# A two-layer retention and attention backbone: its first stage taken feature block by feature block

## The chip, the cores and the metric

The kernel runs on one core of one Trainium2 chip. The metric is the device time of one execution in microseconds (us). Three executions of the kernel before took 2027.63, 2028.96 and 2029.16 us; their median, 2028.96 us, is what the changed kernel is compared with.

Five engines work side by side, each on its own queue of instructions in order: TensorE (PE in the profile, with its weight loads shown apart as PEld), VectorE (DVE), ScalarE (ACT), GpSimd (POOL) and SyncE (SP), which here issues nearly all the transfers (DMAs). [...]

## The reference, cut to what matters

The program is two layers of a diffusion backbone over 256 latent tokens and 256 context tokens, 2048 features each. Layer 0 is a retention with 8 heads, layer 1 a windowed attention. Each layer first normalises its input and modulates it with a shift and a scale that come from a product of SiLU(c) with a large matrix `ada_w`:

```python
c_act = jax.nn.silu(c)
cc_act = jax.nn.silu(c_ctx)
for i in range(DEPTH):
    mod_l = c_act @ ada_w[i] + ada_b[i]
    mod_c = cc_act @ ada_w[i] + ada_b[i]
    sh_l, sc_l, gt_l = jnp.split(mod_l, 3, axis=-1)
    sh_c, sc_c, gt_c = jnp.split(mod_c, 3, axis=-1)
    h_l = _rms_norm(x, norm_gain[i]) * (1 + sc_l[:, None]) + sh_l[:, None]
    h_c = _rms_norm(ctx, norm_gain[i]) * (1 + sc_c) + sh_c
    ...
```

The change lies in the first stage of layer 0. There `h` (512 tokens by 2048 features) is made, and the queries and keys of heads 0 and 1 are projected from it. Retention also needs powers of each head's decay, which come from two vectors of 8 logits.

## The kernel before

**Tiling.** Features lie on partitions: 16 feature blocks (`kb`) of 128 features, 512 tokens in the free dimension (0 to 255 latent, 256 to 511 context). `xT` is the input in this form, `hT_h` and `hT_l` are the modulated input split into a high part and a rest. Every large product is three products (`mm3`, lines 124 to 128): high by high, high by rest, rest by high. Weights arrive by `load_w` (lines 117 to 122): a DMA of 512 KB into one of three buffers `wraw`, a cast on ACT that gives `wh` (line 107) and a subtraction on DVE that gives `wl` (line 104).

**Order.** The kernel is written in a framework that keeps the data dependencies and puts each engine's instructions in an order of its own: what was written earlier goes first among what its planner takes to be ready. So the order in the source is a priority, not a sequence, and each engine's queue may mix work from several places. `tc.issue_after(ins)` adds an edge: whatever the block puts on the engine of `ins` is queued behind `ins`.

**The first stage (lines 243 to 359).** SP issues the eight loads of `xT` (512 KB each, line 247) and the packed constants `cst` (line 248). DVE and POOL work out the decays (lines 256 to 287): some thirty small DVE instructions and three powers on POOL. ACT squares the 16 blocks of `xT`, DVE adds the squares up (lines 290 to 297, two buffers `sq`), and `token_rstd` (lines 192 to 204) turns the sum into one factor per token: PE sums over partitions (line 198), DVE and POOL take the power (lines 183 and 189), PE spreads it (line 203), ACT copies it to `rB` (line 299).

Shift and scale come in "strips". A unit is two feature blocks; its matrix columns arrive in four quarters of 1 MB, `araw` (four buffers, line 314). A quarter is four products with only 32 columns of weights each, in full fp32, side by side in the four column groups of PE (line 316). After the fourth quarter ACT copies the sums out (line 321), PE turns them (line 325), DVE adds up the column groups and adds bias and gain (lines 328, 221 and 224), and `modulate` (lines 206 to 215) makes `hT_h` and `hT_l` of both blocks.

The loop of lines 340 to 356 takes eight groups of products per unit: four output blocks `j` of head 0 (c = 0, accumulated over all units in four PSUM tiles `qk0`) and four of head 1 (c = 1, summed in SBUF in `qk1` through ACT or DVE, lines 354 and 356). PSUM has five `acc` tiles, four of which `qk0` holds, and three `pm` tiles; c = 1 uses the one left for `j` = 0 to 2 and a `pm` for `j` = 3. `DUE` puts the four quarters of the next unit ahead of groups 0, 2, 4 and 5 of the unit at hand.

**Behind it.** The eight heads follow (from line 386), each with projections and tasks put between their pieces. The decays are first read in `decays(h)` (lines 460 to 473), by PE on line 463 and by POOL on line 472, a power over 128 by 128 elements.

## Time and profile before

| | us |
|---|---|
| median of three executions | 2028.96 |
| span of the profiled execution | 2027.2 |
| PE busy in it | 1992.9 |
| DVE, ACT, POOL busy | 1151.6, 694.5, 227.5 |
| first instruction of PE | 20.3 |
| first product of the projections | 34.45 |
| last sum into `qk1` (line 356) starts | 161.9 |

The profile shows one execution. A row of a timeline or chain gives the start and the length of a piece of work in us, the engine, the line of the source and the tile written; what stands in brackets is idle time before it and what ended that. `x8` after a row means eight instructions merged. For line 316 one product is two instructions, so a quarter is `x8`.

### The profile page before, as it was taken

How to read it: one execution, taken by the hardware profiler on the slowest of the kernel's cores; microseconds unless marked ns; L12 is line 12 of the kernel's file. 1: busy time of each engine (PE TensorE's matmuls, PEld its weight loads, DVE VectorE, ACT ScalarE, POOL GpSimd, SP SyncE). 2: the span in 40 equal slices, each digit the busy share in tenths (PEclk: the TensorE clock that was granted, in tenths of full speed). 3: DMA queues.
4: the chain of work that ended last, by engine and by line, in shares of the span. 5: the costliest groups of instructions: out<-in, count | busy, mean ns of one | idle time of the engine just before them, and what ended most of it. 6: DMA issues, size and time to landing. Idle time of an engine off the chain costs nothing.

```text
span 2027.2 us, 25622 instructions
## 1 busy us (share of the span) xinstructions
PE 1992.9 (98%) x9776; PEld 1649.8 (81%) x9776; DVE 1151.6 (57%) x2299; ACT 694.5 (34%) x1043; POOL 227.5 (11%) x76
## 2 busy tenths in 40 slices
PE   5999999999999999999999999999999999999999
PEld 2558888888888888888888888888888788889999
DVE  4556323778678688686464254333232665777754
ACT  3224223232232232232232234322221434656643
POOL 6500402203104004004000000000000010000000
PEclk9999999999999999999999999999999899999999
DMA  9873224555556556655654325533333234444446
GB/s 362 332 266 109 93 89 146 183 191 177 182 177 192 172 180 182 186 180 166 203 173 164 114 94 166 186 126 123 105 125 103 95 109 148 143 135 133 145 161 198
DMA packets 113290, 330.15 MB, mean 163 GB/s; under 512 B 12176, under 2 KB 18448, under 8 KB 108944
## 3 DMA queue, kind: packets, MB, share of 16 engines
q1 hardware_dynamic: 103952, 315.94, 48.0%
q10 hardware_dynamic: 9216, 12.59, 1.7%
q8 instruction: 76, 1.25, 0.2%
q14 instruction: 46, 0.38, 0.1%
HBM read 315.90 MB, written 12.58 MB: 162 GB/s over the span
## 4 chain that ended last, share of the span: by engine, by line
PE 94%; DMA 2%; DVE 2%; ACT 1%; issue 1%; POOL 0%; SPq 0%; ACTq 0%; DVEq 0%; POOLq 0%
PE acc L126 28%; PE acc L127 27%; PE acc L128 27%; PE pm L126 2%; PE pm L127 2%; PE pm L128 2%; PE pm L316 2%; DMA wraw<-in_wo 1%; DMA wraw<-uT_d 1%; DVE wl L104 1%; PE pm L756 1%; PE pm L530 1%; ACT wh L107 1%; DVE ssq L297 0%; DMA xT<-in_xT 0%
## 5 line engine op out<-in xcount | busy, mean ns | idle before, releaser
L104 DVE TENSOR_TENSOR wl<-wraw,wh 128x1024 fp32r<-128x1024 f32 x368 | 449.6, 1223 | 649.6 <-ACT wh L107 649.4
L107 ACT CAST wh<-wraw 128x1024 fp32r<-128x1024 f32 x368 | 386.7, 1051 | 980.6 <-PE acc L128 489.5
L126 PE MATMUL acc<-wh,hT_h 128*128 128x512 f32 x1280 | 502.5, 393 | 1.1 <-ACT hT_h L212 1.1
L127 PE MATMUL acc<-wl,hT_h 128*128 128x512 f32 x1280 | 499.4, 390 | 0.0
L128 PE MATMUL acc<-wh,hT_l 128*128 128x512 f32 x1280 | 499.0, 390 | 0.0
L126 PE MATMUL acc<-hT_h,wh 128*128 128x512 f32 (+1 forms) x1264 | 443.5, 351 | 2.6 <-ACT wh L107 1.9
L127 PE MATMUL acc<-hT_l,wh 128*128 128x512 f32 (+1 forms) x1264 | 440.0, 348 | 0.0
L128 PE MATMUL acc<-hT_h,wl 128*128 128x512 f32 (+1 forms) x1264 | 435.5, 347 | 0.0
L409 DVE SCALAR_TENSOR_TENSOR ajunk<-abraw,crow 128x512 bf16<-128x512 f32 x448 | 308.3, 688 | 11.9 <-ACT crow L398 3.5
L126 PEld LDWEIGHTS acc<-hT_h,wh 128*128 128x128 f32 x1264 | 239.6, 190 | 54.7 <-DVE qk L356 7.2
L126 PEld LDWEIGHTS acc<-wh,hT_h 128*128 128x128 f32 x1280 | 241.2, 188 | 50.2 <-ACT hT_h L212 1.5
L128 PEld LDWEIGHTS acc<-wh,hT_l 128*128 128x128 f32 x1280 | 240.6, 188 | 50.3
L127 PEld LDWEIGHTS acc<-wl,hT_h 128*128 128x128 f32 x1280 | 241.1, 188 | 48.4 <-DVE wl L104 0.2
L127 PEld LDWEIGHTS acc<-hT_l,wh 128*128 128x128 f32 x1264 | 239.8, 190 | 32.2 <-issue 4.2
L128 PEld LDWEIGHTS acc<-hT_h,wl 128*128 128x128 f32 x1264 | 239.3, 189 | 31.0 <-issue 0.8
L472 POOL TENSOR_TENSOR dd<-two,dd 128x128 f32<-128x128 f32 x8 | 167.5, 20943 | 601.6 <-DVE dd L470 601.6
L189 POOL TENSOR_TENSOR rs<-ms,mhalf 128x1 f32<-128x1 f32 (+1 forms) x46 | 40.2, 874 | 1024.5 <-DVE ms L183 673.1
L126 PE MATMUL acc<-r_h,wh 128*128 128x512 f32 x176 | 68.5, 389 | 0.0
L127 PE MATMUL acc<-r_l,wh 128*128 128x512 f32 x176 | 68.5, 389 | 0.0
L128 PE MATMUL acc<-r_h,wl 128*128 128x512 f32 x176 | 68.5, 389 | 0.0
L127 PE MATMUL pm<-r_l,r_h 128*128 128x512 f32 (+1 forms) x176 | 65.7, 373 | 0.5 <-DVE r_l L104 0.5
L126 PE MATMUL pm<-r_h 128*128 128x512 f32 (+1 forms) x176 | 66.1, 375 | 0.0
(199 smaller groups left out, 1514.7 us busy)
## 6 DMA issues: line engine op xcount, KB each, us to landing
wraw<-in_w SPq DMA_DIRECT2D x272, 512.0 KB, 3.5
abraw<-in_adaB SPq DMA_DIRECT2D x256, 256.0 KB, 3.3
wraw<-in_wo SPq DMA_DIRECT2D x96, 512.0 KB, 3.5
araw<-in_adaS SPq DMA_DIRECT2D x32, 1024.0 KB, 7.3
uT_d<-ue ACTq DMA_DIRECT2D x32, 256.0 KB, 2.1
wraw<-uT_d SPq DMA_DIRECT2D x16, 512.0 KB, 3.8
xT<-in_xT SPq DMA_DIRECT2D x8, 512.0 KB, 8.5
wraw<-in_xT SPq DMA_DIRECT2D x8, 512.0 KB, 3.7
```

The source lines that it names most:

```text
L104: return nc.vector.tensor_tensor(out=out, in0=a, in1=hi.bitcast(F32), op=ALU.subtract)
L107: nc.scalar.copy(hi, src)
L126: nc.tensor.matmul(ps, lhsT=ah, rhs=bh, start=start, stop=False)
L127: nc.tensor.matmul(ps, lhsT=ah, rhs=bl, start=False, stop=False)
L128: nc.tensor.matmul(ps, lhsT=al, rhs=bh, start=False, stop=stop)
L189: nc.gpsimd.tensor_tensor(out=rs, in0=ms, in1=mhalf.to_broadcast([P, n]), op=ALU.pow)
L316: nc.tensor.matmul(ap_[32 * j:32 * j + 32, :n], lhsT=cpad[:, 4 * g + j, :], rhs=raw[:, j, :n], start=(g == 0), stop=(g == 3))
L409: nc.vector.scalar_tensor_tensor(out=junk, in0=raw, scalar=1.0, in1=crow[:, t, q * 512:(q + 1) * 512], op0=ALU.mult, op1=ALU.mult, accum_o ...
L472: nc.gpsimd.tensor_tensor(out=dd, in0=two.to_broadcast([P, P]), in1=dd, op=ALU.pow)
L530: nc.tensor.transpose(tp[:, q * P:(q + 1) * P], sg[:, q, f * P:(f + 1) * P], ident)
L756: nc.tensor.transpose(tp[:, j * P:(j + 1) * P], st["prob"][:, j, kb * P:(kb + 1) * P], ident)
```

## The change

It rewrites the first stage and the layout of one input; everything from line 361 on is untouched.

- The matrix for shift and scale is laid out by single feature block: `adaS_d[kb]` is 2 MB, in two halves of 1 MB. `ada_products(kb)` loads both halves and issues all 16 products of the block in a row, each over 256 columns instead of 512. `ada_finish(kb)` does the rest in the same PSUM tile.
- The products of block 0, with their two loads, stand ahead of the loads of `xT`, whose last pair is split into two single blocks. The finish of block 0 stands ahead of the squares.
- Block 0 is modulated straight from the PSUM tile of `token_rstd`; the copy to `rB` comes after. The first weights are loaded before that.
- The loop over 64 groups is written out: parts of head 0 (one block each, which is 12 products) and of head 1 (one block at first, then two) alternate with `ada(kb, after)`, whose products are queued on PE behind the last product of the part named.
- `cst` is loaded after the shift and scale weights of block 5 are asked for, and the decays are computed behind the modulation of block 5.

```diff
+        def ada_products(kb):
+            st = strips[kb] = m_tile()
+            for hf in range(2):
+                raw = pa.tile([P, 8, 256], F32, name="araw", tag="araw", bufs=4)
+                nc.sync.dma_start(out=raw, in_=adaS_d[kb, :, 8 * hf:8 * hf + 8, :])
+                for i in range(8):
+                    j = i % 4
+                    nc.tensor.matmul(st[32 * j:32 * j + 32, 0:L], lhsT=cpad[:, 8 * hf + i, :], rhs=raw[:, i, :],
+                                     start=(hf == 0 and i < 4), stop=(hf == 1 and i >= 4))
+
+        def ada_finish(kb):
+            st = strips.pop(kb)
+            ev = wide("ue", "ev", 2)
+            nc.scalar.copy(ev[:, :L], st[:, :L])
+            for b in range(2):
+                nc.tensor.transpose(st[:, L + b * P:L + (b + 1) * P], ev[:, b * P:(b + 1) * P], ident)
+            tv = pb.tile([P, 2, 2], F32, name="tv", tag="tv", bufs=2)
+            nc.vector.reduce_sum(tv, st[:, L:].rearrange("p (b g r) -> p b r g", b=2, g=4)[:, :, 0:2, :], axis=AX.X)
+            for kind in range(2):
+                ada_mod(kind, 0, kb, 1, tv[:, kind:kind + 1, :], sh0, gs0, gt0)
+
+        ada_products(0)
+        xT = pa.tile([P, KB, T], F32, name="xT")
+        for k0, nk in [(2 * i, 2) for i in range(7)] + [(14, 1), (15, 1)]:
+            nc.sync.dma_start(out=xT[:, k0:k0 + nk, :], in_=xT_d[:, k0:k0 + nk, :])
+        ada_finish(0)
...
+        w = {0: load_w(w0_d[0, 0])}
+        bp = token_rstd(pb, [ssq])
+        first_mod = modulate(wide("pt", "ht", 2), xT[:, 0, :], 0, gs0, sh0, bp)
         rB = wide("aacc0", "rB")
-        nc.scalar.copy(rB, token_rstd(pb, [ssq]))
+        nc.scalar.copy(rB, bp)
+
+        def ada(kb, after):
+            with tc.issue_after(after):
+                ada_products(kb)
+            ada_finish(kb)
+            last_mod[0] = modulate(wide("pt", "ht", 2), xT[:, kb, :], kb, gs0, sh0, rB)
...
+        ada(1, part(0, [0]))
+        with tc.issue_after(first_mod):
+            w[1] = load_w(w0_d[3, 0])
+        ada(2, part(1, [0]))
+        part(0, [1])
+        part(1, [1])
+        w[0] = load_w(w0_d[0, 1])
+        ada(3, part(0, [2]))
+        ada(4, part(0, [3]))
+        w[1] = load_w(w0_d[3, 1])
+        ada(5, part(1, [2, 3]))
+        nc.sync.dma_start(out=cst, in_=cst_d)
+        with tc.issue_after(last_mod[0]):
+            decay_powers()
+        for i in range(2, 8):
+            w[0] = load_w(w0_d[0, i])
+            part(0, [2 * i])
+            end = part(0, [2 * i + 1])
+            if i < 7:
+                ada(2 * i + 2, end)
+            w[1] = load_w(w0_d[3, i])
+            end = part(1, [2 * i, 2 * i + 1])
+            if i < 7:
+                ada(2 * i + 3, end)
```

`part(c, kbs)` issues, for the four output blocks `j`, the `mm3` of the blocks `kbs` and, for head 1, the sum into `qk1`, as the loop did; it returns the last product. `decay_powers()` holds lines 256 to 287 unchanged.

More of the change, by code (lines that the diff above doesn't have):

```diff
@@ L26 @@
 LOG2E = 1.4426950408889634
-DUE = (0, 2, 4, 5)
-DUE0 = (0, 2, 4, 5)
 GAP1, GAP2 = 4, 2
@@ L127, in mm3 @@
         nc.tensor.matmul(ps, lhsT=ah, rhs=bl, start=False, stop=False)
-        nc.tensor.matmul(ps, lhsT=al, rhs=bh, start=False, stop=stop)
+        return nc.tensor.matmul(ps, lhsT=al, rhs=bh, start=False, stop=stop).ins
     def gemm_ws(w_d, chunk, nkp, moving, n, hook=None, pre=None, tail=1):
@@ L212, in modulate @@
             nc.scalar.activation(hT_h[:, kb, c], t[:, c], AF.Identity, bias=sh[:, kb, s:s + 1])
-            nc.vector.scalar_tensor_tensor(out=hT_l[:, kb, c], in0=t[:, c], scalar=sh[:, kb, s:s + 1],
-                                           in1=hT_h[:, kb, c].bitcast(F32), op0=ALU.add,
-                                           op1=ALU.subtract)
+            last = nc.vector.scalar_tensor_tensor(out=hT_l[:, kb, c], in0=t[:, c], scalar=sh[:, kb, s:s + 1],
+                                                  in1=hT_h[:, kb, c].bitcast(F32), op0=ALU.add,
+                                                  op1=ALU.subtract)
+        return last.ins
     def ada_mod(kind, layer, k0, nk, src, sh, gs, gt, ntk=2):
@@ L241, in wide, with decay_powers @@
         return pb.tile([P, 512], F32, name=name, tag=tag, bufs=bufs)
-    with tc.tile_pool(name="pa", bufs=1) as pa:
-        xT = pa.tile([P, KB, T], F32, name="xT")
-        for i in range(8):
-            nc.sync.dma_start(out=xT[:, 2 * i:2 * i + 2, :], in_=xT_d[:, 2 * i:2 * i + 2, :])
-        nc.sync.dma_start(out=cst, in_=cst_d)
-        nc.scalar.activation(cact.rearrange("p k t -> p (k t)"), vec[:, V_C:V_C + 32], AF.Silu)
-        cpad = wide("aacc1", "cpad").rearrange("p (k t) -> p k t", t=32)
-        nc.gpsimd.memset(cpad, 0.0)
-        nc.vector.tensor_copy(cpad[:, :, 0:2], cact)
+    def decay_powers():
         xl = vec[:, V_LGT:V_LGT + 16]
@@ L287, in backbone @@
                                 in1=sixt.to_broadcast([P, 64]), op=ALU.mult)
+    with tc.tile_pool(name="pa", bufs=1) as pa:
+        cpad = wide("aacc1", "cpad").rearrange("p (k t) -> p k t", t=32)
+        nc.gpsimd.memset(cpad, 0.0)
+        nc.scalar.activation(cact.rearrange("p k t -> p (k t)"), vec[:, V_C:V_C + 32], AF.Silu)
+        nc.vector.tensor_copy(cpad[:, :, 0:2], cact)
+        strips, last_mod = {}, [None]
+        def ada_products(kb):
[22 more added lines that the diff above has]
+        ada_finish(0)
         ssq = wide("rows", "ssq")
@@ L297, in backbone @@
             nc.vector.tensor_tensor(out=ssq, in0=ssq, in1=sq, op=ALU.add)
+        w = {0: load_w(w0_d[0, 0])}
+        bp = token_rstd(pb, [ssq])
+        first_mod = modulate(wide("pt", "ht", 2), xT[:, 0, :], 0, gs0, sh0, bp)
         rB = wide("aacc0", "rB")
-        nc.scalar.copy(rB, token_rstd(pb, [ssq]))
-        units = [[2 * k, 2 * k + 1] for k in range(8)]
-        strips = {}
-        def strip_part(u, g):
-            kbs = units[u]
-            n, c0 = 256 * len(kbs), 256 * (kbs[0] % 2)
-            if g == 0:
-                strips[u] = m_tile()
-            ap_ = strips[u]
-            raw = pa.tile([P, 4, 512], F32, name="araw", tag="araw", bufs=4)
-            nc.sync.dma_start(out=raw[:, :, :n], in_=adaS_d[kbs[0] // 2, g][:, :, c0:c0 + n])
-            for j in range(4):
-                nc.tensor.matmul(ap_[32 * j:32 * j + 32, :n], lhsT=cpad[:, 4 * g + j, :],
-                                 rhs=raw[:, j, :n], start=(g == 0), stop=(g == 3))
-            if g < 3:
-                return
-            ev = wide("ue", "ev", 2)
-            nc.scalar.copy(ev[:, :n], ap_[:, :n])
-            tp = m_tile()
-            nb = n // P
-            for b in range(nb):
-                nc.tensor.transpose(tp[:, b * P:(b + 1) * P], ev[:, b * P:(b + 1) * P], ident)
-            tv = pb.tile([P, 2, 2, 2], F32, name="tv", tag="tv", bufs=2)
-            nc.vector.reduce_sum(tv.rearrange("p k n t -> p (k n) t")[:, :nb, :],
-                                 tp[:, :n].rearrange("p (b g r) -> p b r g", b=nb, g=4)[:, :, 0:2, :], axis=AX.X)
-            for kind in range(2):
-                ada_mod(kind, 0, kbs[0], len(kbs), tv[:, :len(kbs), kind, :], sh0, gs0, gt0)
-            for kb in kbs:
-                modulate(wide("pt", "ht", 2), xT[:, kb, :], kb, gs0, sh0, rB)
@@ L336, in backbone @@
+        nc.scalar.copy(rB, bp)
[4 more added lines that the diff above has]
+            last_mod[0] = modulate(wide("pt", "ht", 2), xT[:, kb, :], kb, gs0, sh0, rB)
         qk0 = [acc_tile() for _ in range(4)]
         qk1 = pb.tile([P, 4, 512], F32, name="qk1", tag="sg")
-        due = [(8 * (u - 1) + (DUE if u > 1 else DUE0)[g], u, g) for u in range(8) for g in range(4)]
-        w = {}
-        for n in range(64):
-            while due and due[0][0] <= n:
-                strip_part(*due.pop(0)[1:])
-            kbs, c, j = units[n // 8], n % 8 // 4, n % 4
-            if j == 0 and kbs[0] % 2 == 0:
-                w[c] = load_w(w0_d[3 * c, kbs[0] // 2])
-            wh, wl = w[c]
-            ps = qk0[j] if c == 0 else (m_tile() if j == 3 else acc_tile())
-            js = slice(j * P, (j + 1) * P)
-            for kb in kbs:
-                mm3(ps, (wh[:, kb % 2, js], wl[:, kb % 2, js]), h_mov(kb),
-                    start=(kb == 0 if c == 0 else kb == kbs[0]),
-                    stop=(kb == KB - 1 if c == 0 else kb == kbs[-1]))
-            if c == 1 and n < 8:
-                nc.scalar.copy(qk1[:, j, :], ps)
-            elif c == 1:
-                nc.vector.tensor_tensor(out=qk1[:, j, :], in0=ps, in1=qk1[:, j, :], op=ALU.add)
@@ new lines, in part @@
+        def part(c, kbs):
+            for j in range(4):
+                wh, wl = w[c]
+                ps = qk0[j] if c == 0 else (m_tile() if j == 3 else acc_tile())
+                js = slice(j * P, (j + 1) * P)
+                for kb in kbs:
+                    last = mm3(ps, (wh[:, kb % 2, js], wl[:, kb % 2, js]), h_mov(kb),
+                               start=(kb == 0 if c == 0 else kb == kbs[0]),
+                               stop=(kb == KB - 1 if c == 0 else kb == kbs[-1]))
+                if c == 1 and kbs[0] == 0:
+                    nc.scalar.copy(qk1[:, j, :], ps)
+                elif c == 1:
+                    nc.vector.tensor_tensor(out=qk1[:, j, :], in0=ps, in1=qk1[:, j, :], op=ALU.add)
+            return last
@@ L867, in _layout @@
     aw = i["ada_w"]
-    s = np.concatenate([np.concatenate([aw[0][:, 128 * k:128 * k + 128],
-                                        aw[0][:, 2048 + 128 * k:2048 + 128 * k + 128]], 1) for k in range(16)], 1)
-    a["adaS"] = _pieces(s, 4)
+    s = aw[0][:, :4096].reshape(16, 128, 2, 16, 128)
+    a["adaS"] = np.ascontiguousarray(s.transpose(3, 1, 0, 2, 4).reshape(16, 128, 16, 256))
     s = np.concatenate([aw[0][:, 4096:], aw[1]], 1).T
```

## The prediction

> **What bounds the kernel now.** I read the page first: span, busy times, the chain of work that ended last.

> ```profile
> span 2027.2 us, 25622 instructions
> PE 1992.9 (98%) x9776; PEld 1649.8 (81%) x9776; DVE 1151.6 (57%) x2299; ACT 694.5 (34%) x1043; POOL 227.5 (11%) x76
> ...
> PE 94%; DMA 2%; DVE 2%; ACT 1%; issue 1%; POOL 0%; SPq 0%; ACTq 0%; DVEq 0%; POOLq 0%
> ```

> PE is the bound: the reader should see that only 34.3 us of the span have no PE work in them (2027.2 - 1992.9). The busy times by window say where those lie.

> ```profile
> 235.00:700.00 465.00, 465.00 (x2104) 385.16 (x2103) 298.25 (x686) 136.60 (x200) 79.89 (x20) 1.00 0.53 165
> 700.00:1300.00 600.00, 599.47 (x2701) 495.74 (x2700) 358.05 (x775) 191.54 (x295) 53.53 (x18) 1.00 0.53 167
> ```

> Behind the first stage PE has no idle time to speak of, so whatever the first stage saves or loses arrives at the end one for one. The chain of the first 36 us shows the front of the stage.

> ```profile
> 1.65 6.43 DMA xT<-in_xT
> 8.10 0.64 ACT sq L296
> 8.76 0.70 DVE ssq L297
> 9.56 0.69 DVE ssq L297
> 10.25 0.10 DVE t L266
> 10.35 0.69 DVE ssq L297
> ...
> 19.59 0.70 DVE ssq L297
> 20.34 1.88 PE pm L198 x8
> ...
> 22.50 1.01 POOL rs L189
> 23.55 1.11 PE pm L203 x4
> 24.66 4.84 PE pm L316 x32
> 29.53 0.59 ACT ev L321
> 30.17 0.67 PE pm L325 x4
> ...
> 31.63 0.50 DVE ht L210
> 32.15 1.31 ACT hT_h L212 x3
> ...
> 34.45 0.80 PE acc L126
> ```

> Until 20.3 the sum of squares on DVE ends last, not the loads; then the token factor, then unit 0's strip of 4.84 us, and the first product starts at 34.45. From there PE is nearly saturated; only two short waits close the stage.

> ```profile
> 148.65 0.50 PE L126 MATMUL acc<-hT_h,wh 128*128 128x512 f32 x1 [0.30 <-DVE qk L356]
> ...
> 150.66 0.97 PE L126 MATMUL acc<-hT_h,wh 128*128 128x512 f32 x3 [0.34 <-ACT hT_h L212]
> ```

> **The change, part by part.** *Start of the products.* Block 0's 2.10 MB now go ahead of the tokens. The transfers' view over the first 45 us, in 40 slices of 1.125 us, gives the rate; the view of tile xT the landings.

> ```profile
> GB/s 0 48 327 364 295 364 306 393 408 408 430 415 433 435 429 430 430 422 422 408 437 277 44 22 117 291 415 401 437 430 430 415 401 448 426 437 415 430 382 411
> ...
> 1.18 4.87 SPq L247 DMA_DIRECT2D xT<-in_xT  x8
> ...
> DMA to landing us min/median/max: 3.8/8.5/10.3
> ```

> Eight slices move 2.36 MB by 9.0 us, which is `vec` (480 columns, 0.25 MB) and block 0. Bytes are counted before a transfer has landed: the eight token loads (4.44 MB with `vec`) are moved by 14.0 but the last, issued just before 6.05, lands 10.3 later, near 15.8. I add these 1.7 us: block 0 has landed at about 10.6, the first token pair (0.52 MB at 420 GB/s, 1.25 us) at 11.9, the last block near 20.6. The squares cannot follow at that rate: before, adds follow each other in 0.79 us at the fastest (9.56 to 10.35), 0.83 on average with the decays in between ((19.59 - 8.76) / 13). So the chain starts at 11.9, takes two squares (1.2 us) and 15 adds of 0.79 (11.9) and ends at 25.0; the copy and four small DVE instructions of `ada_finish(0)` cost some 0.3 in between: 25.3, against 20.3. The strip left the path, but the loads ahead of the tokens push the tokens back 5 us. From there it is as before: 4.32 us to the end of the spread (20.34 to 24.66), then 1.4 us for one `ht` and two of the three `hT_h` (31.63 to 32.15 + 0.87), 0.1 for the releases: first product at **31.2**, bounds 30.0 (no cost in between, no decays on DVE) and 33.5 (the copy goes ahead of the first square, 0.9, and the cast of the first weights, 1.05 on ACT, between two squares). The weights hide: their load stands right behind the tokens, lands near 22, and cast and rest fit before 29.7. Gain 34.45 - 31.2 = **3.25**.

> *Strips.* Their price per quarter, and its parts:

> ```profile
> 67.59 0.99 PE pm L316 x8
> 68.58 0.43 PE acc L126
> 69.02 0.24 PE acc L127
> ...
> 80.23 0.44 PE pm L325 x4
> ...
> 31.48 1.07 PE L316 MATMUL pm<-araw,cpad 128*32 128x512 f32 x8 [0.66 <-DMA araw<-in_adaS]
> ...
> 28.42 0.12 PEld L316 LDWEIGHTS pm<-araw,cpad 128*32 128x32 f32 x4 [0.31 <-issue]
> ...
> 61.68 0.69 DVE L356 TENSOR_TENSOR qk<-acc,qk 128x512 f32<-128x512 f32 x1 [6.50 <-PE acc L128]
> ```

> A quarter costs 0.99 and makes the next product 0.19 longer: 1.19 (rounded up). In a running strip four instructions side by side take 0.12 + 0.31 = 0.43 (512 columns), so two such groups are 0.86 and 0.33 is the price of switching to and fro. Ahead of the first product unit 0 (32 instructions from 24.66 on) and one quarter of unit 1 (from 31.48) are done, so 27 of the 32 quarters follow: 32.1 us. After: 15 blocks of eight groups with 256 columns. Such a group does not occur; I take half, 0.215, since the loads of weights (0.12) lie beside the products: 1.72 + 0.33 = 2.05, 15 times 30.75. Gain **1.4**. Bounds: loads not hidden at half the length give 0.335 a group, 0.96 more a block, 14.4 us lost; no price for the switch gives 5.0 more. 0.215 lies nearest, because the transposes, with full-width loads, also run in 0.11 each.

> *Transposes*: 28 of 0.11 before (0.44 for four), 30 after: **-0.2**. Sums, bias and gain on DVE double in number (some 0.7 us a block at instructions of 0.16 to 0.2), beside PE work, DVE being 57% busy.

> *The order of blocks.* A strip's end to both `hT_h` halves took 29.53 to 33.02, 3.5 us; I take 3.4 for a block. Each part of one head and one block is 12 products, 2.8 us. From 31.2: part 0 of block 0 with seven products at half clock until 35.4 (below), strip 1, part 1 of block 0, strip 2 (through 40.9), both parts of block 1, part 0 of block 2 (through 50.9), strip 3 (through 53, with the turn of strip 2). Part 0 of block 3 needs strip 3's result at 56.2; what is ready meanwhile is only one or two output blocks of head 1 for block 2 (1.4 us), since one `acc` is free and strip 4 is queued behind the part that waits. A hole of 56.2 - 53.1 - 1.4 = **-1.7**; bounds 0 and -3.3. From block 4 on each strip has 4.2 us or more of other products between its end and its use, if the `pm` output block of head 1 is issued early as now, so no hole. The loads keep up: a pair of blocks costs 48 products of 0.235, two strips and four transposes, 15.8 us, and a block's buffers come free when the strip two blocks before ends, 13.7 ahead of its own; its 2.1 MB are 5 us at 420 GB/s, 11.3 with another block and a pair of weights ahead in the queue. What stands behind a waiting load on SP is only weights of a later part. Four more sums into `qk1`, on one `acc` tile: 0.69 each, of which products of other tiles hide all or nothing (0 to 2.8); I take **-0.3**, as the 28 of now cost one wait of 0.30. The closing waits go, as the last strip is done a part earlier: **+0.65**.

> *Clock.* The windows' columns are the stretch, its length, PE's busy time and instructions, the granted clock, the share of DMA and GB/s.

> ```profile
> 34.00:35.00 1.00, 0.55 (x1) 0.50 0.99 418
> ...
> 37.00:38.00 1.00, 1.00 (x5) 0.83 1.02 418
> ```

> The first products run at half clock until about 37.3, some seven of them. In the changed kernel PE has done still less ahead of its first product, so I give it the same half clock for as long: no difference, +-1.

> *Decays and constants.* Moved: about thirty DVE instructions of 0.17 us, three powers on POOL, one transfer of 288 KB, past the modulations of blocks 1 to 5.

> ```profile
> 24.16 10.52 POOL L284 TENSOR_TENSOR gam<-two,gam 128x64 f32<-128x64 f32 x1 [0.66 <-DVE gam L281]
> ...
> 35.77 41.59 POOL L472 TENSOR_TENSOR dd<-two,dd 128x128 f32<-128x128 f32 x2
> ...
> 189.19 0.44 PE pm L463 x4
> ```

> By the sum above block 5 is modulated near 68 (strip 5 ends near 65). The logarithm took less than 24.2 us before, as the powers start there; the two powers of the decays 11.6 (24.16 to 35.77), line 472 41.6. So POOL is done by 146, and the first reader on PE comes at 189. Cover 43 us; beyond it each us would count in full. Cost 0. No product hangs on the small DVE instructions, and the modulation has the 4.2 us named above to wait behind them.

> ```profile
> L104 DVE TENSOR_TENSOR wl<-wraw,wh x5: 1218/1224/1226, 39.9 to 71.1; 128x1024 fp32r<-128x1024 f32 x5
> ...
> L104 DVE TENSOR_TENSOR wl<-wraw,wh x8: 1215/1216/1218, 86.4 to 136.9; 128x1024 fp32r<-128x1024 f32 x8
> ```

> While POOL ran line 472 the subtraction for `wl` took 1.224 us, afterwards 1.216: no blocking. [...]

> *Sum*: 3.25 + 1.4 - 0.2 - 1.7 - 0.3 + 0.65 = 3.1. Against the profiled 2027.2 that is a span of 2024.1; the median lies 1.76 above the span, and I take it to stay so: 2028.96 - 3.1 = **2025.9**.

> **The rivals.** A change under 0.2%, 4.1 us, is about what a measurement of this kernel cannot tell from none.

> 1. *Faster, no hole.* The planner fills the hole and ACT and DVE take nothing between the squares: 3.1 + 1.7 + 1.2 = 6 us, **2023.0**. For it: the order now fills every gap of head 1. Against: strip 4 is held behind the waiting part.
> 2. *Slower, weight loads show.* With 256 columns the four loads no longer lie beside the products: 14.4 lost, **2040.3**. Place: every strip. It decides above 0.215 + 3.1 / 120 = 0.24 us a group. Against: 0.12 is well under 0.215.
> 3. *A hole in every pair.* If strip 5, 7, ... end up behind all of head 1's products, the next part of head 0 covers 2.8 of 3.4 us: 0.6 in five pairs, and the full 3.3 at block 3: **2030.5**. The same time comes about where the change does not do what it says and the halves of a strip are split by other products: 15 more switches of 0.33 are 5.0.
> [...]

> **How the numbers follow.** Forecast (gain 0 to 4.1) 0.40; rival 1 0.36; rival 3 0.11, of which 0.03 with still longer holes are beyond 0.2%; rival 2 0.10; rival 4 0.03. Faster by over 0.2%: 0.36. Within: 0.40 + 0.08 = 0.48. Slower: 0.03 + 0.10 + 0.03 = 0.16. The forecast's own range is 2024.9 to 2029.0. The range for 8 in 10 goes from 2019 (rival 1 with most of the switch's 5.0) to 2034 (rival 3 with the late start, 33.5); left out are rivals 2 and 4.

> **What would show it.** First product at 31.2, last add of line 297 ending near 25.3; 32 strip instructions in 1.7 us with nothing between; PE idle near 53 to 56 ahead of block 3; last sum into `qk1` about 3 us earlier than 161.9; POOL's powers over before 140. Wrong would be: tokens that land before 18, groups over 0.24 us, or idle time of PE at every second block.

## The result, and the profile after

The changed kernel took 2043.64 us (median of 4 executions, 2043.00 to 2044.23), the kernel before beside it 2028.70 us (4 executions, 2027.63 to 2029.16). The ratio is 1.0074, with a 95% interval of 1.0061 to 1.0086: **slower by 15 us**, and outside the predicted range.

The page of the changed kernel begins with its span and busy times:

```profile
span 2041.7 us, 26211 instructions
PE 2001.3 (98%) x10032; PEld 1661.0 (81%) x10032; DVE 1162.4 (57%) x2335; ACT 694.9 (34%) x1051; POOL 228.1 (11%) x76
```

The span grew by 14.5 us. PE is busy 8.4 us longer (2001.3 - 1992.9), and the other 6.1 are idle. So there are two sorts of loss: PE does its work more slowly, and it waits. The chain of waits over the first 60 us shows the front:

```profile
23.79 0.70 DVE ssq L324
...
26.69 1.95 POOL rs L187
...
31.31 1.65 PE acc L124 x3
...
48.86 0.92 ACT hT_h L210 x2
49.82 0.72 PE acc L124 x2
...
58.36 0.92 ACT hT_h L210 x2
59.32 0.80 PE acc L124
```

The first product starts at 31.31, where 31.2 was forecast: the gain ahead of the products is there. It is lost behind them. The last sum into `qk1`, at 161.93 before, now starts at 178.55 (timeline of DVE):

```profile
178.55 0.68 DVE L353 TENSOR_TENSOR qk<-pm,qk 128x512 f32<-128x512 f32 x1
```

From first product to last sum it is 147.24 us against 127.48: **19.8 us lost in the stage**. PE's timeline (start, length, work; in brackets the idle time before it) shows three kinds of loss within 30 us:

```profile
59.32 1.65 PE L124 MATMUL acc<-hT_h,wh 128*128 128x512 f32 x3 [2.26 <-ACT hT_h L210]
...
63.62 1.93 PE L294 MATMUL pm<-araw,cpad 128*32 128x256 f32 x32
65.48 0.50 PE L124 MATMUL acc<-hT_h,wh 128*128 128x512 f32 x1
...
68.69 0.62 PE L294 MATMUL pm<-araw,cpad 128*32 128x256 f32 x2
69.24 0.50 PE L124 MATMUL acc<-hT_h,wh 128*128 128x512 f32 x1
...
70.84 1.07 PE L294 MATMUL pm<-araw,cpad 128*32 128x256 f32 x16
71.84 0.50 PE L124 MATMUL acc<-hT_h,wh 128*128 128x512 f32 x1
...
73.42 1.06 PE L294 MATMUL pm<-araw,cpad 128*32 128x256 f32 x14
74.42 0.50 PE L124 MATMUL acc<-hT_h,wh 128*128 128x512 f32 x1
...
86.85 0.79 PE L126 MATMUL acc<-hT_h,wl 128*128 128x512 f32 x1 [2.97 <-DVE wl L102]
```

*Cut strips.* Strip 4 (at 63.62) runs whole: 1.86 from its start to the next product, and the products on either side of it together take some 0.2 longer, so 2.05, as forecast. Strip 5 comes in three pieces of 2, 16 and 14 instructions with six products between each two: 0.55, 1.00 and 1.00 to the next product, each plus the 0.2, so 3.15. Seven of the 15 strips (2, 5, 7, ... 15) are cut like this: 8 x 2.05 + 7 x 3.15 = 38.5 us, against 30.75 forecast and 32.1 before.

*Holes.* PE waits 1.16 for block 2 (49.82), 0.55 + 2.26 for block 3, 2.97 for `wl` at 86.85, and 0.2 in each of five later pairs: 7.9 us in all, against 0.65 before.

*Half clock.* Behind two of these holes the granted clock is halved. The windows of after (stretch, its length, PE busy and instructions, then the other engines, the granted clock, DMA share, GB/s):

```profile
55.45:58.86 3.41, 1.06 (x14) 0.33 (x6) 1.45 (x6) 0.87 (x3) 0.00 (x0) 1.00 0.73 238
58.86:62.28 3.42, 2.96 (x7) 2.39 (x8) 2.11 (x3) 1.34 (x3) 0.00 (x0) 0.50 0.99 413
82.76:86.17 3.41, 1.12 (x7) 0.70 (x5) 2.94 (x15) 0.37 (x1) 0.00 (x0) 1.00 0.91 320
86.17:89.58 3.41, 2.73 (x7) 2.15 (x8) 3.31 (x17) 1.18 (x3) 0.00 (x0) 0.50 0.98 410
89.58:93.00 3.42, 3.42 (x8) 1.68 (x7) 1.79 (x6) 0.75 (x1) 3.07 (x1) 0.50 0.10 42
```

Seven products behind the first hole and eleven behind the second run at 0.43 instead of 0.235 (18 x 0.195 = 3.5), and one piece of a strip takes 0.99 instead of 0.55: about 4 us. Together: strips 6.4 (38.5 - 32.1), holes 7.2 (7.9 - 0.65), clock 4.0, so 17.6 of the 19.8. Another 0.4 lies at the start, where nine products run at 0.43 (31.31 to 35.17) and before there were seven (34.45 to 37.48). The rest, some 2, is not placed by these rows.

Why `wl` was late is read from DVE's timeline:

```profile
78.67 0.17 DVE L251 TENSOR_SCALAR ax<-ax 128x16 f32<-128x16 f32 x1
81.86 0.17 DVE L253 TENSOR_SCALAR t<-e 128x16 f32<-128x16 f32 x1 [3.02 <-POOL e L252]
...
85.49 0.17 DVE L260 TENSOR_SCALAR lacc<-lacc 128x16 f32<-128x16 f32 x1
85.58 1.22 DVE L102 TENSOR_TENSOR wl<-wraw,wh 128x1024 fp32r<-128x1024 f32 x1
```

The decays' small instructions wait 3.02 us for a power on POOL and then run one after the other, one every 0.21 us. In DVE's queue they stand ahead of the subtraction for the next weights. From the start of the wait (78.84) to that subtraction it is 6.7 us.

### The profile page after: what moved, and what is told of

The parts are those of the page before. It is cut to its first block, busy times and chain, and to the rows that moved or that the text cites. A ratio compares the mean times of both kernels' runs of the same rounds, so it can differ in the third digit from the quotient of the medians.

```text
span 2041.7 us, 26211 instructions
## 1 busy us (share of the span) xinstructions
PE 2001.3 (98%) x10032; PEld 1661.0 (81%) x10032; DVE 1162.4 (57%) x2335; ACT 694.9 (34%) x1051; POOL 228.1 (11%) x76
## 4 chain that ended last, share of the span: by engine, by line
PE 95%; DVE 2%; DMA 1%; ACT 1%; issue 1%; POOL 0%; SPq 0%; DVEq 0%; POOLq 0%; ACTq 0%
PE acc L124 28%; PE acc L125 28%; PE acc L126 27%; PE pm L125 2%; PE pm L126 2%; PE pm L124 2%; PE pm L294 2%; DMA wraw<-uT_d 1%; PE pm L780 1%; PE pm L554 1%; DVE ssq L324 1%; DVE wl L102 0%; ACT hT_h L210 0%; DMA araw<-in_adaS 0%; ACT wh L105 0%
## 5 line engine op out<-in xcount | busy, mean ns | idle before, releaser
L126 PE MATMUL acc<-wh,hT_l 128*128 128x512 f32 x1280 | 498.9, 390 | 0.0
L126 PE MATMUL acc<-hT_h,wl 128*128 128x512 f32 (+1 forms) x1264 | 437.9, 348 | 3.0 <-DVE wl L102 3.0
L126 PEld LDWEIGHTS acc<-wh,hT_l 128*128 128x128 f32 x1280 | 240.6, 188 | 50.3
L126 PEld LDWEIGHTS acc<-hT_h,wl 128*128 128x128 f32 x1264 | 240.3, 190 | 33.6 <-DVE wl L102 3.2
L126 PE MATMUL acc<-r_h,wl 128*128 128x512 f32 x176 | 68.5, 389 | 0.0
## 6 DMA issues: line engine op xcount, KB each, us to landing
xT<-in_xT SPq DMA_DIRECT2D x7, 512.0 KB, 10.3
```

Of the source, the lines that this page charges most:

```text
L126: return nc.tensor.matmul(ps, lhsT=al, rhs=bh, start=False, stop=stop).ins
```

## The experiments

Every edit from 1 to 6 is on top of the changed kernel; 7 to 9 join them. Ratios are against the kernel before, run beside each (its medians lie between 2027.67 and 2028.67), with their 95% intervals. "Stage" is the time from first product to last sum into `qk1`: 147.24 in the changed kernel.

**1. Decays back at the head.**

```diff
             nc.sync.dma_start(out=xT[:, k0:k0 + nk, :], in_=xT_d[:, k0:k0 + nk, :])
+        nc.sync.dma_start(out=cst, in_=cst_d)
+        decay_powers()
         ada_finish(0)
...
-        nc.sync.dma_start(out=cst, in_=cst_d)
-        with tc.issue_after(last_mod[0]):
-            decay_powers()
```

> The changed kernel (2043.6 us) with the decays and the load of the constants put back to where they were before the change, right behind the token loads; all else as changed. Theory A (the decays' wait for POOL in VectorE's queue holds up the subtraction for wl, PE idles 2.97 us at 86.85 and then runs 6.8 us at half clock): about 6 us are won, 2037 to 2038, and the idle time near 87 and the half clock behind it are gone. Rival B (the late decays only fill time that is lost anyway, to the strips cut in pieces): 2043 to 2044. Beside it a small cost: the small instructions between the squares make the first product some 0.5 us later.

Measured: 1.0102 (1.0088 to 1.0115), slower still. The stage shrank by 5.5, to 141.7, what theory A has for the hole near 87 (2.97) and the half clock behind it (about 2.6). But the time forecast by theory A was missed by over 10 us, for a reason that the chain of waits shows:

```profile
23.94 0.21 DVE gam L268 x2
24.22 10.91 POOL gam L271
35.20 0.29 POOL gam L273
35.49 0.97 POOL rs L187
```

POOL took the long power of the decays ahead of the short one of the token factor, and the first product came at 40.66. The same kind of mistake, an in-order queue, moved to another engine. So this run shows the hole's cause but not its price.

**2. Strips kept whole.** Strips 5, 7, ... queued behind the last product of head 1's third output block (`last2[0]`):

```diff
-        ada(5, part(1, [2, 3]))
+        part(1, [2, 3])
+        ada(5, last2[0])
...
-            end = part(1, [2 * i, 2 * i + 1])
+            part(1, [2 * i, 2 * i + 1])
             if i < 7:
-                ada(2 * i + 3, end)
+                ada(2 * i + 3, last2[0])
```

> The changed kernel with one edit: the strips of blocks 5, 7, 9, 11, 13 and 15 are queued on PE behind the last product of output block j=2 of head 1 instead of j=3, so that nothing of that part is left to cut them in pieces of 2, 16 and 14 instructions. Theory A (each cut strip costs two more switches, about 1.1 us): 6 strips, 6 to 7 us won, 2037. Rival B (the pieces only fill the waits of head 1 for its one acc tile, which then show as idle time): 2042 to 2045. Rival C (the strip comes later by two output blocks, and the product of the next block but one waits for it): slower than 2045, with waits on hT_h in every pair.

Measured: 1.0092 (1.0078 to 1.0105), no better. Apart from strip 2, the strips were whole, but PE's idle time in the stage rose from 7.9 to 14.4 us. The view of PE's waits has a row that the changed kernel does not have (total, times, longest):

```profile
PE acc L124 <- DVE qk L355: 4.0, 7, 1.2
```

Head 1's outputs `j` = 0, 1, 2 share one PSUM tile, so each must wait until DVE has taken the one before. The pieces of the strip had been filling just these waits. Forbidding the cut takes the filling away and leaves the wait: the cut is a symptom. These 4.0 are the larger part of the 6.5 us of new idle time (rival B). Of the rest, 2.0 are longer waits for `hT_h` (6.4 against 4.4), as rival C had it.

**3. Strips 3 and 4 one part earlier.**

```diff
-        part(0, [1])
+        ada(3, part(0, [1]))
         part(1, [1])
         w[0] = load_w(w0_d[0, 1])
-        ada(3, part(0, [2]))
-        ada(4, part(0, [3]))
+        ada(4, part(0, [2]))
+        part(0, [3])
```

> The changed kernel with strips 3 and 4 queued one part of one block earlier (3 behind part 0 of block 1, 4 behind part 0 of block 2). Theory A (block 3 waits for a strip that starts too late; 2.8 us idle and 3.4 us of half clock follow): 4 us won, 2039 to 2040, no half clock near 59. Rival B (the strip's weights, asked for when block 1's buffers come free at 37, land only at 47 and the hole moves ahead of the strip): 2042 to 2044.

Measured: 1.0062 (1.0049 to 1.0074), median 2040.12. The hole of 2.26 ahead of block 3 and its half clock are gone (the longest wait for `hT_h` is 1.5); idle time fell to 5.0 us, 3.5 of it in the wait for `wl`, which stayed with its 6.83 us of half clock. That is theory A.

**4. Tokens ahead of block 0's weights.** `ada_products(0)` moved behind the nine loads of `xT`.

> The changed kernel with block 0's two weight loads behind the token loads instead of ahead of them. Theory A (the squares are paced by VectorE from the landing of the first tokens, and strip 0 fits beside them): the sum of squares ends near 20, the first product starts near 26.5 to 27 instead of 31.3, 4 to 5 us won: 2039. Rival B (the strip's chain, from weights that land near 21, ends last, or the loads of block 1 and the first weights come late): start at 29 or later, 2041 to 2044.

Measured: 1.0062 (1.0048 to 1.0075), median 2039.53. The first product came at 29.97, not at 26.5 to 27: the second half of strip 0 now ran only behind the spread of the token factor, and in DVE's timeline the subtraction of the first weights stood between the two halves of block 0:

```profile
27.37 1.22 DVE L102 TENSOR_TENSOR wl<-wraw,wh 128x1024 fp32r<-128x1024 f32 x1
28.50 0.48 DVE L211 SCALAR_TENSOR_TENSOR hT_l<-ht,sh,hT_h 128x256 fp32r<-128x256 f32 x1
28.90 0.48 DVE L208 SCALAR_TENSOR_TENSOR ht<-xT,gs,pm 128x256 f32<-128x256 f32 x1
```

So only 1.3 us came from the start, which is rival B's; that the time is theory A's is luck. Of the rest, part is the clock: the half clock behind the wait for `wl` shows as 3.41 us (82.96 to 86.37) instead of 6.83.

**5. The decays in two parts.** Logarithms (up to `lg2`) at the head, where DVE waits for data anyway; the long powers `gam` on POOL behind the token factor's (`last_rs[0]`).

```diff
         nc.vector.tensor_copy(cpad[:, :, 0:2], cact)
+        decay_logs()
...
         ada(2, part(1, [0]))
+        nc.sync.dma_start(out=cst, in_=cst_d)
+        with tc.issue_after(last_rs[0]):
+            decay_powers()
...
-        nc.sync.dma_start(out=cst, in_=cst_d)
-        with tc.issue_after(last_mod[0]):
-            decay_powers()
```

> The changed kernel (2043.6 us) with the decays in two pieces: the logarithms at the head of the kernel, as before the change, and the two powers on POOL queued behind the token factor's power (the constants are loaded behind the weights of block 2). Theory A (the late decays cost the 2.97 us wait of the subtraction for wl and the half clock behind it; in e1 the same was won in the middle, 147.2 to 141.7 us from the first product to the last sum into qk1, and lost at the start to the power of 10.9 us ahead of the token factor on POOL): first product within 1 us of 31.3, the stage as short as in e1, 2037 to 2038. Rival B (any early decays delay the squares or the token factor): first product at 33 or later, 2040 or more.

Measured: 1.0049 (1.0034 to 1.0063), median 2038.67. No wait for `wl` beyond 0.2 us, and behind block 3's hole the products run at 0.23 from the start; the last sum starts at 172.27 although the first product came 0.7 later. POOL ran its long powers from 44 to 96, in the middle of the stage:

```profile
44.08 10.52 POOL L274 TENSOR_TENSOR gam<-two,gam 128x64 f32<-128x64 f32 x1 [14.71 <-DVE gam L271]
...
54.92 41.42 POOL L500 TENSOR_TENSOR dd<-two,dd 128x128 f32<-128x128 f32 x2
```

It is thus not POOL's work that hurt, but the place of the small instructions in DVE's queue. Of the 5 us won, 1.4 have another source: the half clock behind block 3's hole is gone as well, though the hole is still there (last section).

**6. A second tile for head 1.**

```diff
-                ps = qk0[j] if c == 0 else (m_tile() if j == 3 else acc_tile())
+                ps = qk0[j] if c == 0 else (m_tile() if j % 2 else acc_tile())
```

> The changed kernel with one edit: head 1's output blocks take the acc tile and a pm tile in turn (j = 0, 2 and j = 1, 3) instead of acc for j = 0, 1, 2. Theory A (the strips are cut in pieces because the planner fills with them the time in which head 1 waits for its one acc tile; a cut strip costs 3.15 us, a whole one 2.05): the strips of blocks 5, 7, 9, 11, 13, 15 are whole and no idle time takes their place, 6 to 7 us won, 2037. Rival B (as in e2, whole strips leave waits of about the same length): 2043 to 2046.

Measured: 1.0043 (1.0030 to 1.0056), median 2037.71. All strips but the second stay whole, without any order being forced, and the last sum comes at 170.85, 7.7 earlier. No idle time takes the place of the cuts: it is 7.2 us, block 3's hole (2.3) and the wait for `wl` (3.25) above all, and behind the latter products run at 0.43 from 87.12 to 90.55. Why strip 2 is still cut, this run does not show. PE's timeline, strip 5 behind head 1's products:

```profile
71.68 0.39 PE L126 MATMUL pm<-hT_h,wl 128*128 128x512 f32 x1
72.00 1.93 PE L294 MATMUL pm<-araw,cpad 128*32 128x256 f32 x32
73.86 0.50 PE L124 MATMUL acc<-hT_h,wh 128*128 128x512 f32 x1
```

**7. Both (5 and 6).**

> e5 and e6 together. If the two causes are separate, their gains add up: 2043.6 - 6 - 6.5 = 2031. If they share time (the wait near 87 also depends on the tiles), 2034 or more.

Measured: 1.0019 (1.0010 to 1.0028), median 2032.71. The last sum comes at 166.22. The two gains add up as measured: 5.0 in experiment 5, 5.9 in 6, 10.9 here, of the 15 lost. The 2031 expected had put both a little higher.

**8. All four (7, 3 and 4).**

> e7 with block 3's strip one part earlier (e3) and block 0's weights behind the tokens (e4). The pieces added up: 2031 - 3.5 - 4 = 2023.5, faster than the kernel before by 4 us. If e3 and e4 won their time from the same idle time and half clock, 2027 to 2029.

Measured: 0.9992 (0.9983 to 1.0001), median 2027.55: level with the kernel before. Behind the first product PE idles 0.4 us up to the end of the stage, and the last sum starts at 160.31 (161.93 before). The four edits together undo the loss. The single gains do not add up here (2023.5): experiment 3 had won the half clock behind block 3's hole, as 5 had, and 4 half of that behind the wait for `wl`, which 7 removes by itself as 5 does. It is the second case of the expectation. What is left of the change's idea shows in the chain of waits:

```profile
20.02 1.81 PE pm L198 x8
...
23.16 0.90 PE pm L203 x3
24.07 1.91 PE pm L298 x16
...
28.29 1.22 DVE wl L102
...
30.89 0.80 PE acc L124
```

Strip 0 and the subtraction of the first weights still stand at the wrong places of their queues.

**9. And the front in order.** On top of 8; `last_hi` and `last_lo` are cast and subtraction of the first weights, `end0` is the last product of strip 0, and `token_rstd` queues its spread behind it:

```diff
-        bp = token_rstd(pb, [ssq])
-        first_mod = modulate(wide("pt", "ht", 2), xT[:, 0, :], 0, gs0, sh0, bp)
+        with tc.issue_after(last_hi[0]), tc.issue_after(last_lo[0]):
+            ada_finish(0)
+        bp = token_rstd(pb, [ssq], end0)
+        with tc.issue_after(last_lo[0]):
+            first_mod = modulate(wide("pt", "ht", 2), xT[:, 0, :], 0, gs0, sh0, bp)
```

> The fourth kernel of this series with everything undone, and three more edges ahead of the first product: the spread of the token factor is queued behind block 0's strip, and the finish and the modulation of block 0 behind cast and subtraction of the first weights. In the kernel before this one the second half of the strip had landed at 20.45 but ran at 24.07, behind the spread, and the subtraction of 1.22 us stood at 28.29 between the two halves of block 0; the first product came at 30.89. Theory A (what is saved ahead of the first product arrives at the end one for one): strip done by about 23.8, spread by 24.9, first product at 27.5 to 28, last sum into qk1 near 157.5, span near 2023, time near 2024.5, a ratio near 0.998 against the kernel before. Rival B (the loads take the place): the weights of blocks 1 and 2 land no earlier than now, so the products wait for them or the half clock lasts longer; first product near 28, but last sum near 160 and the time near 2027.5 as without the edges.

Measured: 0.9985 (0.9976 to 0.9994), median 2025.29 against 2028.13: **faster than both kernels**, than the one before by only 0.15%, with an interval that just leaves out 1. The chain of waits:

```profile
19.11 1.80 PE pm L198 x8
20.91 1.86 PE pm L303 x16
22.77 1.05 PE pm L208 x4
...
26.49 1.65 PE acc L124 x3
```

The strip runs while DVE and POOL work out the token factor; the first product comes at 26.49 and the last sum at 157.40, both earlier than theory A had them. Of the 4.4 us of earlier start 2.9 reach the last sum: strip 2 was cut again and 0.9 us more of small waits showed. The span fell by 2.3.

## Why the prediction was wrong

- **Start of the products: right, in part by luck.** 3.25 us forecast, 3.14 measured (34.45 to 31.31). Two errors cancelled: the squares ended at 24.5 rather than 25.3, and POOL's power for the token factor took 1.95 instead of 1.01.
- **Price of a strip: right; number of strips in one piece: wrong.** 2.05 us whole was exact, and the four side by side on 256 columns did cost half (32 instructions take 1.86 and 16 take 1.00, so four take 0.215), so rival 2 falls. The step that failed is "15 times 30.75". The prediction had a cut as rival 3's second form ("halves of a strip are split by other products", 5.0 us), tied to the change not doing what it says. The cost was 7.7: 14 more switches, of 0.55 each where 0.33 was put. The price depends on where the cut falls. In experiment 8 strips 3 and 4 run as two pieces of 16 and cost 2.40 each, 0.35 more than whole; the piece of 2 in the changed kernel costs another 0.75. What sets the number of cuts is not the change's bursts but head 1's single PSUM tile: the planner takes anything ready to fill the wait. Experiments 2 and 6 show it from both sides for six of the seven strips; for strip 2 it stays open.
- **Order of the blocks: right place, wrong size.** The hole ahead of block 3 was put at 1.7, because 1.4 us of head 1's products were to fill it. They did not, and block 2 had a hole too: 1.16 + 0.55 + 2.26 = 4.0, and 1.4 of half clock behind it. Half clock behind a hole in the stage was not priced at all ("no difference, +-1" spoke of the start alone).
- **From block 4 on: nearly right.** No large hole; 0.2 us in each of five pairs where none was forecast.
- **Decays at no cost: wrong, the second large miss.** The cover that was named, 43 us from POOL's powers to their reader, held: the powers were done at 142.8 and first read at 205.17. The failing sentence is "No product hangs on the small DVE instructions, and the modulation has the 4.2 us named above to wait behind them". It looked at the modulation only; the subtraction for the next weights also stands behind them. And it left out that these instructions wait for POOL themselves. Cost: 2.97 of waiting and about 2.6 of half clock.
- **Rival 4, given 0.03 (POOL's powers hold up DVE): no run shows it.** In the changed kernel the long powers run from 89.93 to 142.8, and the six subtractions for `wl` between 97.32 and 137.6 take 1.22 to 1.23 us, as the one at 85.58 does with POOL idle (1.22). In experiment 5 the powers lie in the middle of the stage, and PE waits 0.2 us for `wl`.
- **Behind the stage one for one: nearly.** The last sum came 16.6 late, the span 14.5. Some of the difference is a later stretch at half clock, near 1600 us in both kernels, which lasts 10.24 us before and 6.83 after.

On paper the change's gain was 3.1 us. Start and whole strips were as forecast; cut strips, two holes with their clock, and the decays took some 18 back.

## What to carry to other kernels

Where work is moved, list everything that stands *behind* it in its engine's in-order queue, small instructions included, and whether the moved work itself waits for another engine; a far-away reader of its result is no cover for what is queued behind it. A burst is only worth its burst price if nothing next to it waits: give the wait its second buffer first, and the planner has no reason to cut the burst. Price a hole of PE with the half clock that may follow it, here 2.6 us behind one of 2.97 and 1.4 behind one of 2.26.

## What the runs showed of the hardware

```profile
55.24:58.65 3.41, 2.28 (x34) 1.04 (x34) 0.88 (x5) 0.37 (x1) 3.41 (x1) 1.00 0.38 86
58.65:62.06 3.41, 1.74 (x8) 1.44 (x9) 2.74 (x6) 1.84 (x3) 3.41 (x1) 1.00 1.00 423
62.06:65.48 3.42, 3.42 (x40) 1.98 (x39) 0.40 (x1) 0.16 (x1) 3.42 (x1) 1.00 0.70 273
```

The border falls into the hole, and in neither window is PE busy for less than 1.74 of 3.41 us. In the changed kernel the windows ahead of the two drops have 1.06 and 1.12. In experiment 3 a window with the same 1.74 was followed by half clock:

```profile
78.26:81.67 3.41, 1.74 (x14) 0.77 (x6) 2.86 (x17) 0.37 (x1) 0.00 (x0) 1.00 0.85 288
81.67:85.08 3.41, 1.59 (x4) 1.30 (x5) 3.31 (x17) 0.45 (x1) 0.20 (x1) 0.50 0.98 408
```

So 1.74 went both ways, and PE's busy time in a window does not by itself tell the clock of the next; one with 1.87 was followed by the full clock in experiment 2 (84.96 to 88.38). Of the windows at half clock, those with 2.96 (58.86 to 62.28) and, in the kernel before, 2.89 (33.92 to 37.34) were followed by the full clock, one with 2.73 (86.17 to 89.58) by a second one at half. What decides between them, these runs do not show.

One thing stays open: the token factor's power on POOL, the same 128 by 4 elements, took 1.95 us in the changed kernel and 1.93 in experiment 5, but 1.01 before and in experiments 8 and 9. A power that had run before it does not explain this: experiment 5 had one and took 1.93, experiment 4 had none and took 1.03. The cause stays open.
